# RWKV-7 recurrence inside a fused decoder layer: the second head's rows and columns swapped, its small matmuls put on the opposite quarters of the array, and the values' share of each chunk made one chunk ahead

## The chip, the cores and the metric

The kernel runs on one core of a Trainium2 chip. The metric is the device time of one execution in microseconds (us).

## What is computed

One decoder layer, in float32: sequence 1024, model width 1024. The input goes through an RMS norm and one input projection; its columns feed an RWKV-7 branch (8 heads of 64), an S5 branch and two gates; the two branches are projected, gated, merged and projected out; then a gated MLP. Most of the matrix work is large projections. The part that the change touches is the RWKV-7 recurrence:

```python
def step(S, inp):
    r_t, w_t, k_t, v_t, a_t, b_t = inp
    sa = jnp.einsum('bhij,bhj->bhi', S, a_t)
    S = (S * w_t[:, :, None, :] + sa[..., None] * b_t[:, :, None, :]
         + v_t[..., None] * k_t[:, :, None, :])
    return S, jnp.einsum('bhij,bhj->bhi', S, r_t)
```

The kernel doesn't run it step by step but in chunks of 64 steps. For one head and one chunk, with the decays folded into the factors, let A be the rows of `a` and R those of `r`, B and K the rows of `b` and `k`, V the values. Four 64x64 products of (A, R) with (B, K) make the Gram block `gr`. The block of A with B is triangular and is inverted; U solves the triangular system whose right side is A·S plus the share of the values (A·K)·V; the output is R·S + (R·B)·U + (R·K)·V; and S grows by B·U + K·V, which is one product with the stacked `UV`.

## The kernel before

**Groups and heads.** The eight heads are four pairs of pairs: the work is cut into four groups i = 0 to 3 (two groups of four heads, times two halves `th` of the sequence). In a group, `u` (0, 1) counts the two pairs of heads and `h` (0, 1) the two heads of a pair: head h of a pair holds its 64 channels on partitions 64h to 64h+63.

**Stages of a group.** `rwkv_front(d, u)` (L641) loads k, r, v and the two gates of a pair, and makes `ar` (the rows of A in columns 0 to 63 and of R in 64 to 127 of every chunk), `bk` (B and K likewise) and, with the Gram matmuls of L700 and the masking of L702, `gr`. VectorE makes the A half (L685) and the B half (L688), GpSimd the R half (L686) and the K half (L691, after its L689 and L690); VectorE's L709 makes the factor of the bonus out of the result of GpSimd's L690. `rwkv_inv` (L744) gathers the diagonal blocks of `gr` to DRAM and back (L707, L750, L762, L770, all DMAs issued on GpSimd's queue) and inverts 32x32 blocks on VectorE (L757, L759). `rwkv_nat` (L717) transposes `bk` and the values into `bkn` and the lower half of `UV`. `rwkv_level` (L772) joins the 32x32 inverses into 64x64 ones by small matmuls, L783 and L786. `rwkv_chain` (L798) runs the eight chunks, each with three segments of small matmuls:

- segment 1: L814, four products `ar`·S with a 64x128 tile of the array (64 rows of contraction, 128 columns of output; the heads use the upper and the lower row half), then L816, four products `gr`·`UV` on a 128x64 tile that add the values' share; ScalarE's L818 copies the result to `p1`;
- segment 2: L824, four 64x64 products of `gr` with `p1`, all on the same quarter; VectorE's L825 copies U into `UV`;
- segment 3: L828, four products for the output, and L832, four for the state; ScalarE's L830 copies the output to `yn`, VectorE's L835 updates S.

`rwkv_out` (L838) normalizes the output per head (VectorE, L867 last) and transposes it (L873).

**What sets the order.** TensorE's order is written by hand: `drive` (L184) interleaves three lanes, `chain_lane` (nat, level, chain, out of one group) and `prep_lane(0)`, `prep_lane(1)` (front of the next group; the second also inverts), with a background of large projections, `mm3_steps`, whose matmuls stand in L171, L172 and L173 (128x128 weights, 512 columns, three per step; called "fill" below). A lane yields the cost of what it has just issued and the time until its next step is due. Costs, pace and due times are numbers of a plan, not measured times. A lane that is not due, or whose credit is used up, lets fill steps through. When the order has been made it is fixed: TensorE runs it as written and waits where an operand isn't there. The order on the other engines comes from a scheduler that works from the same program and priorities, and every engine runs its own queue in order.

A float32 matmul shows as two instructions ("passes") in the trace, so four matmuls are a row of x8.

## Time and profile before

| | |
|---|---|
| median of three runs | 1645.7 us (1644.71 to 1648.14) |
| the profiled execution, its own time | 1647.22 us |
| its span, first to last instruction | 1645.4 us |
| mean granted TensorE clock in it | 0.963 |
| TensorE busy | 1552.2 us, 94% of the span |
| VectorE, ScalarE, GpSimd busy | 1129.1, 701.0, 146.2 us |
| RWKV stage (first matmul L666 to last transposes L873) | 278 to 846 us of the span |

Times in the trace count from the span's start. In a timeline, a row gives the start, the time from its first to its last instruction, the engine, line and operation, output<-inputs, the array tile that a matmul uses (rows*columns), the shape and count, and in brackets how long the engine had been idle before it and what ended that. Rows of neighbouring matmuls overlap, since a matmul's record lasts until its result is written, while the next one has long begun: the spacing of starts, not the length of a row, is what a matmul costs.

### The profile page before, as it was taken

What the parts mean: (1) busy time and instruction counts of PE and PEld (TensorE: products, weight loads), DVE (VectorE), ACT (ScalarE), POOL (GpSimd) and SP (SyncE); (2) the same over time, 40 slices, a digit from 0 to 9 for tenths busy, and PEclk for the clock granted to TensorE, in tenths of its full rate; (3) what the DMA queues carried; (4) which work ended last, traced back from release to release, by engine and by line L of the source; (5) the groups of instructions that cost most, each with busy time, mean ns of one, the idle gap of its engine ahead of it and who ended that gap; (6) DMA issues with size and microseconds to landing.
All of it is one profiled execution on the core that took longest, in us unless ns stands there. A gap on an engine that the chain in (4) does not pass through costs nothing. (4 is left out here: it accounts for less than half of the span.)

```text
span 1645.4 us, 22661 instructions
## 1 busy us (share of the span) xinstructions
PE 1552.2 (94%) x8372; PEld 1251.5 (76%) x8372; DVE 1129.1 (69%) x2035; ACT 701.0 (43%) x1069; POOL 146.2 (9%) x212
## 2 busy tenths in 40 slices
PE   5899899899999999989989899999999999999995
PEld 4688787687777777767778688878888888788774
DVE  6898764554364364695378668977777777788767
ACT  4345543123243243535453444544444544543451
POOL 2100101312212213111010000000000000000000
PEclk9799999998997998999999999999999999999997
DMA  5254243333333334655257344422222224862722
GB/s 174 71 146 143 88 141 136 98 115 110 94 119 103 94 119 133 156 146 156 59 174 248 128 150 151 140 92 78 77 90 78 80 96 145 296 234 86 235 89 102
DMA packets 130399, 212.59 MB, mean 129 GB/s; under 512 B 38080, under 2 KB 44224, under 8 KB 130288
## 3 DMA queue, kind: packets, MB, share of 16 engines
q1 hardware_dynamic: 120464, 181.50, 35.1%
q0 software_dynamic: 8672, 27.54, 5.5%
q10 hardware_dynamic: 1152, 2.10, 0.3%
q8 instruction: 66, 1.08, 0.3%
q14 instruction: 45, 0.37, 0.1%
HBM read 156.03 MB, written 52.95 MB: 127 GB/s over the span
## 5 line engine op out<-in xcount | busy, mean ns | idle before, releaser
L171 PE MATMUL gm<-hh,wh 128*128 128x512 f32 x688 | 301.6, 438 | 7.4 <-ACT hh L225 3.5
L172 PE MATMUL gm<-hl,wh 128*128 128x512 f32 x688 | 279.3, 406 | 5.4 <-DVE hl L226 4.5
L173 PE MATMUL gm<-hh,wl 128*128 128x512 f32 x688 | 278.5, 405 | 0.0
L156 DVE TENSOR_TENSOR wl<-wf,wh 128x512 fp32r<-128x512 f32 x179 | 123.2, 689 | 142.3 <-ACT wh L155 141.5
L155 ACT CAST wh<-wf 128x512 fp32r<-128x512 f32 x179 | 110.7, 619 | 205.3 <-PE gm L172 115.1
L171 PEld LDWEIGHTS gm<-hh,wh 128*128 128x128 f32 x688 | 134.4, 195 | 44.3 <-ACT hh L225 5.7
L172 PEld LDWEIGHTS gm<-hl,wh 128*128 128x128 f32 x688 | 135.3, 197 | 31.7 <-DVE hl L226 7.3
L173 PEld LDWEIGHTS gm<-hh,wl 128*128 128x128 f32 x688 | 134.7, 196 | 29.7
L1514 PE MATMUL d<-xl,wh 128*128 128x512 f32 x308 | 120.4, 391 | 5.7 <-DVE xl L226 5.7
L1513 PE MATMUL d<-xh,wh 128*128 128x512 f32 x308 | 120.1, 390 | 0.0
L1515 PE MATMUL d<-xh,wl 128*128 128x512 f32 x308 | 119.9, 389 | 0.0
L1339 PE MATMUL rp<-t,h 128*128 128x512 f32 x216 | 84.4, 391 | 2.3 <-ACT p L1353 1.4
L1341 PE MATMUL rp<-t,l 128*128 128x512 f32 x216 | 84.2, 390 | 0.5 <-DVE l L226 0.5
L1340 PE MATMUL rp<-t,h 128*128 128x512 f32 x216 | 84.0, 389 | 0.0
L1514 PEld LDWEIGHTS d<-xl,wh 128*128 128x128 f32 x308 | 57.8, 188 | 19.6 <-DVE xl L226 7.8
L1513 PEld LDWEIGHTS d<-xh,wh 128*128 128x128 f32 x308 | 57.8, 188 | 12.0 <-ACT q L1574 0.2
L1515 PEld LDWEIGHTS d<-xh,wl 128*128 128x128 f32 x308 | 57.8, 188 | 12.0
L225 ACT CAST h<-r 128x1024 fp32r<-128x1024 f32 x34 | 35.8, 1054 | 61.1 <-PE rp L1340 29.6
L226 DVE TENSOR_TENSOR l<-r,h 128x1024 fp32r<-128x1024 f32 x34 | 41.6, 1225 | 29.0 <-ACT h L225 27.5
L1360 DVE SCALAR_TENSOR_TENSOR y<-zv,vecs,y 128x1023 f32<-128x1023 f32 (+1 forms) x36 | 46.1, 1281 | 8.6 <-ACT y L1358 8.6
L1339 PEld LDWEIGHTS rp<-t,h 128*128 128x128 f32 x216 | 40.5, 188 | 11.8 <-ACT p L1353 2.3
L1341 PEld LDWEIGHTS rp<-t,l 128*128 128x128 f32 x216 | 40.5, 188 | 9.4 <-DVE l L226 1.0
(440 smaller groups left out, 3381.8 us busy)
## 6 DMA issues: line engine op xcount, KB each, us to landing
r<-in_w_up_dram SPq DMA_DIRECT2D x36, 512.0 KB, 3.6
wf<-in_w_in_dram SPq DMA_DIRECT2D x68, 256.0 KB, 3.0
st<-in_w_down_dram SPq DMA_DIRECT2D x55, 256.0 KB, 4.1
st<-ACT SPq DMA_DIRECT2D x44, 256.0 KB, 4.5
wf<-in_w_up_dram SPq DMA_DIRECT2D x36, 256.0 KB, 2.8
ACT<-y POOLq DMA_DIRECT2D x18, 512.0 KB, 2.9
GT<-ev SPq DMA_DIRECT2D x32, 256.0 KB, 2.1
wf<-in_w_br_dram SPq DMA_DIRECT2D x32, 256.0 KB, 3.1
```

The lines of the kernel that those rows point to most:

```text
L155: nc.scalar.copy(h[:, :n], f[:, :n])
L156: nc.vector.tensor_tensor(l[:, :n], f[:, :n], h[:, :n].bitcast(F32), ALU.subtract)
L171: mm(ps, a, xh[k], start=k == 0, stop=False)
L172: mm(ps, a, xl[k], start=False, stop=False)
L173: mm(ps, b, xh[k], start=False, stop=k == n - 1)
L1339: mm(ps, wh[:, c], xh, start=first and k == 0, stop=False, skip_group_check=True)
L1340: mm(ps, wh[:, c], xl, start=False, stop=False, skip_group_check=True)
L1341: mm(ps, wl[:, c], xh, start=False, stop=k == 3, skip_group_check=True)
L1360: V.scalar_tensor_tensor(y[:, lag:], z[:, 0:1024 - lag], self.vec(nme, i), y[:, lag:], ALU.mult, ALU.add)
L1513: mm(ps, wh[:, c], xh[:, x], start=start, stop=False, skip_group_check=True)
L1514: mm(ps, wh[:, c], xl[:, x], start=False, stop=False, skip_group_check=True)
L1515: mm(ps, wl[:, c], xh[:, x], start=False, stop=stop, skip_group_check=True)
```

## The change

For head 1 (h = 1) the two column halves of `ar`, `bk` and `gr` and the two row halves of `UV` change places: A, B and U of head 1 lie where R, K and V of head 0 lie. So a product of head 0 that uses rows 0 to 63 and columns 0 to 63 has a partner of head 1 on rows 64 to 127 and columns 64 to 127. The mask `gmask` is widened to 192 columns to serve both.

- In the front, each of the four operations that make `ar` and `bk` is cut into two, one for each head, on 64 partitions each (L688, L689, L694, L695 of the new kernel); the gather L707 and the scatter L770 become eight DMAs a group each in place of four.
- In `rwkv_nat`, the copy of the values to `UV` becomes two, a small matmul is added for the first block, and the memset of `UV` goes.
- In `rwkv_level`, the matmuls alternate between the two heads (two 32x32 tiles).
- In the chain, `ar`·S is made in two halves. Segment 1 now has the half for A (L838, four 64x64) and the values' share of the next chunk (L820, four 64x64); ScalarE's L824 keeps that share, and VectorE's L841 adds the kept share of this chunk to `ar`·S, in place of ScalarE's copy L818. Segment 2 has the four products of `gr` with `p1` (L849) and the half of `ar`·S for R (L851). Segment 3 has the four products with `UV` for the output (L856) and four for the state (L861). That is 24 matmuls a chunk for 20, all but segment 3's on 64x64 tiles. U is copied to `UV` by VectorE (L852) for head 0 and by ScalarE (L853) for head 1. A segment of four `values` matmuls is added before the first chunk.
- The plan's costs of the segments go from 1.25, 0.5 and 0.9 to 0.45, 0.45 and 0.65, those of the level from 0.4 to 0.3; so the places of all fill steps in the stage change. The number of fill matmuls doesn't.

```diff
         o = slice(d["th"] * 512, d["th"] * 512 + 512)
         p = 2 * d["g"] + u
         ar, bk = d["ar"][:, u], d["bk"][:, u]
-        ar0, ar1, bk0, bk1 = ar[:, :, 0:64], ar[:, :, 64:128], bk[:, :, 0:64], bk[:, :, 64:128]
+        ar0, ar1, bk0, bk1 = [[x[HS[h], :, HS[h ^ j]] for h in range(2)] for x in (ar, bk) for j in range(2)]
 
         gf = d["gr"][:, u].rearrange("p c h t -> p (c h t)")
         kk, yb, pe = gf[:, 0:512], gf[:, 512:1024], gf[:, 1024:1544].rearrange("p (c t) -> p c t", t=65)
@@ -682,29 +684,32 @@
         for tb in range(4):
             nc.tensor.transpose(kb[:, tb * 128:(tb + 1) * 128], yb[:, tb * 128:(tb + 1) * 128], self.cst("ident"))
         V.scalar_tensor_tensor(kk, k, self.vec("k_k", p), kb, ALU.mult, ALU.mult)
-        V.scalar_tensor_tensor(ar0, c64(kk), -1.0, pe[:, :, 0:64], ALU.mult, ALU.mult)
-        G.tensor_tensor(ar1, c64(r), pe[:, :, 1:65], ALU.mult)
+        for h, sl in enumerate(HS):
+            V.scalar_tensor_tensor(ar0[h], c64(kk)[sl], -1.0, pe[sl, :, 0:64], ALU.mult, ALU.mult)
+            G.tensor_tensor(ar1[h], c64(r)[sl], pe[sl, :, 1:65], ALU.mult)
         V.scalar_tensor_tensor(kk, ta, 1.0, kk, ALU.add, ALU.mult)
-        V.scalar_tensor_tensor(bk0, c64(kk), 0.5, c64(tz), ALU.mult, ALU.mult)
         G.tensor_scalar(ta, ta, self.ka_h[:, p:p + 1], self.ka_1[:, p:p + 1], ALU.mult, ALU.add)
         G.tensor_tensor(ta, ta, k, ALU.mult)
-        G.tensor_tensor(bk1, c64(ta), c64(tz), ALU.mult)
+        for h, sl in enumerate(HS):
+            V.scalar_tensor_tensor(bk0[h], c64(kk)[sl], 0.5, c64(tz)[sl], ALU.mult, ALU.mult)
+            G.tensor_tensor(bk1[h], c64(ta)[sl], c64(tz)[sl], ALU.mult)
         v = ld(self.RKV[8 + p])
...
-        g16 = d["gr"][:, u].rearrange("p c h t -> p (c h) t")
         for blk in range(2):
-            sl = slice(32 * blk, 32 * blk + 32)
-            nc.gpsimd.dma_start(d["md"][u, blk].rearrange("c q t -> q c t"), g16[sl, :, sl])
+            md = d["md"][u, blk].rearrange("(c h) q t -> h q c t", h=2)
+            for h in range(2):
+                sl = slice(64 * h + 32 * blk, 64 * h + 32 * blk + 32)
+                nc.gpsimd.dma_start(md[h], d["gr"][sl, u, :, h, sl])
...
                     if b == 0:
                         mm(ps[64:128, c], v[:, 0:64], ident, start=True, stop=True, skip_group_check=True)
+                        mm(ps[0:64, c], v[:, 448:512], ident, start=True, stop=True, skip_group_check=True)
                     else:
                         nc.tensor.transpose(ps[:, c], v[:, 64 * b - 64:64 * b + 64], ident)
-                A.copy(d["UV"][64:128, 4 * q:4 * q + 4, :, u], ps[64:128].rearrange("p c (h i) -> p c h i", i=64))
+                for h in range(2):
+                    A.copy(d["UV"][HS[1 - h], 4 * q:4 * q + 4, h, u], ps[HS[1 - h], :, HS[h]])
...
+        kw = dict(stop=True, skip_group_check=True)
+        steps = ((lambda u, c, h: mm(p1[u][bot[h], c], gr[top[h], u, c, h, bot[h]], xz[top[h], u, c], start=c == 0, **kw),
+                  lambda u, h: A.copy(xz[bot[h], u], p1[u][bot[h], 0:8])),
+                 (lambda u, c, h: mm(p0[u][top[h], c], xz[bot[h], u, c], gr[bot[h], u, c, h, bot[h]], start=c == 0, **kw),
+                  lambda u, h: A.copy(gr[top[h], u, :, h, bot[h]], p0[u][top[h], 0:8])))
         for step, evict in steps:
             for u in range(2):
-                for c in range(16):
-                    step(u, c)
-                    if c % 8 == 7:
-                        yield 0.4, 0.3, 2.0
-                evict(u)
+                for c in range(8):
+                    for h in range(2):
+                        step(u, c, h)
+                    if c % 4 == 3:
+                        yield 0.3, 0.3, 2.0
+                for h in range(2):
+                    evict(u, h)
             yield 0, T_LV
     def rwkv_chain(self, d):
@@ -802,38 +809,59 @@
         S, pt, UV, gr, ar, bkn = self.S[d["g"]], d["pt"], d["UV"], d["gr"], d["ar"], d["bkn"]
         d["yn"] = self.tg("yn", 1, (128, 4, 2, 2, 64))
         kw = dict(stop=True, skip_group_check=True)
-        uh = [(u, h) for h in range(2) for u in range(2)]
+        uh = [(u, h, HS[h], HS[1 - h]) for u in range(2) for h in range(2)]
+
+        def banks():
+            t = self.chk(1).rearrange("p (b e u i) -> p b e u i", b=2, u=2, i=64)
+            return t[:, 0, 0], t[:, 1, 0], t[:, 1, 1]
+
+        def values(pg, c, u):
+            for _, h, sl, ot in uh[0:2]:
+                mm(pg[sl, u], gr[ot, u, c, h, sl], UV[ot, (c + h) % 8, h, u], start=u == 0, **kw)
+
+        def keep(pg):
+            t = self.small.tile([128, 2, 64], F32, tag="p1", name=self.nm("p1"), bufs=2)
+            A.copy(t, pg)
+            return t
+        _, pg, _ = banks()
+        for u in range(2):
+            values(pg, 0, u)
+        nxt = keep(pg)
+        yield 0.3, 0
         for c in range(8):
-            py = self.chk(1).rearrange("p (h n) -> p h n", h=2)[:, :, 0:128].rearrange("p h (u i) -> p h u i", i=64)
+            pa, pg, py = banks()
+            p1 = nxt
             cb = self.chb()
-            pu = cb[0:64, 0:256].rearrange("p (h u i) -> p h u i", u=2, i=64)
-            psn = cb[:, 256:384].rearrange("p (u i) -> p u i", i=64)
+            pu, psn = [cb[:, o:o + 128].rearrange("p (u i) -> p u i", i=64) for o in (0, 256)]
             for u in range(2):
-                for h in (1, 0):
-                    sl = slice(64 * h, 64 * h + 64)
-                    mm(py[:, h, u], ar[sl, u, c], S[sl, u], start=u == 0, **kw)
-            for u, h in uh:
-                mm(py[0:64, h, u], gr[:, u, c, h, 0:64], UV[:, c, h, u], start=False, **kw)
-            p1 = self.small.tile([64, 2, 2, 64], F32, tag="p1", name=self.nm("p1"), bufs=1)
-            A.copy(p1, py[0:64])
+                for _, h, sl, ot in uh[0:2]:
+                    mm(pa[sl, u], ar[sl, u, c, sl], S[sl, u], start=u == 0, **kw)
+                if c < 7:
+                    values(pg, c + 1, u)
+            V.tensor_tensor(p1, p1, pa, ALU.add)
+            if c < 7:
+                nxt = keep(pg)
             spt = self.small.tile([128, 2, 64], F32, tag="spt", name=self.nm("spt"), bufs=1)
             for u in range(2):
                 A.mul(spt[:, u], S[:, u], pt[:, c, u:u + 1])
-            yield 1.25, T_CH
-            for j, (u, h) in enumerate(uh):
-                mm(pu[:, h, u], gr[0:64, u, c, h, 0:64], p1[:, h, u], start=j == 0, **kw)
-            V.tensor_copy(UV[0:64, c], pu)
-            yield 0.5, T_CH
-            for u, h in uh:
-                mm(py[64:128, h, u], gr[:, u, c, h, 64:128], UV[:, c, h, u], start=False, **kw)
+            yield 0.45, T_CH
+            for u, h, sl, ot in uh:
+                mm(pu[sl, u], gr[sl, u, c, h, sl], p1[sl, u], start=u == 0, **kw)
+            for u, h, sl, ot in uh:
+                mm(py[ot, u], ar[sl, u, c, ot], S[sl, u], start=c == 7 and u == 0, **kw)
+            V.tensor_copy(UV[0:64, c, 0], pu[0:64])
+            A.copy(UV[64:128, (c + 1) % 8, 1], pu[64:128])
+            yield 0.45, T_CH
+            for u, h, sl, ot in uh:
+                mm(py[ot, u], gr[:, u, c, h, ot], UV[:, (c + h) % 8, h, u], start=False, **kw)
             o = 64 * (c % 2)
-            A.copy(d["yn"][o:o + 64, c // 2].rearrange("p u h i -> p h u i"), py[64:128])
-            for u, h in uh:
-                mm(psn[64 * h:64 * h + 64, u], bkn[:, u, c, 64 * h:64 * h + 64], UV[:, c, h, u],
-                   start=u == 0 and h == 1, **kw)
+            for h in range(2):
+                A.copy(d["yn"][o:o + 64, c // 2, :, h], py[HS[1 - h]])
+            for u, h, sl, ot in uh:
+                mm(psn[sl, u], bkn[:, u, c, sl], UV[:, (c + h) % 8, h, u], start=False, **kw)
             for u in range(2):
                 V.scalar_tensor_tensor(S[:, u], psn[:, u], pt[:, c, u:u + 1], spt[:, u], ALU.mult, ALU.add)
-            yield 0.9, T_CH
+            yield 0.65, T_CH
```

**TensorE, second and third chunk of group 0 beside the front of group 1.** These are the rows before, from the third segment of the second chunk (L828, L832) on; `gm` is the output of a fill step, `rp` that of the Gram matmuls L700, `chk` and `chb` those of the chain.

```order
1313 L828 MATMUL chk_3627<-UV_3235,gr_2468 64x64 x4
1314 L832 MATMUL chb_3628<-UV_3235,bkn_3234 64x64 x4
1315 L700 MATMUL rp_3670<-ar_3332,bk_3333 128x128
...
1322 L700 MATMUL rp_3671<-ar_3332,bk_3333 128x128
1323 L171 MATMUL gm_3620<-hh_514,wh_3476 128x512
1324 L172 MATMUL gm_3620<-hl_515,wh_3476 128x512
1325 L173 MATMUL gm_3620<-hh_514,wl_3477 128x512
1326 L814 MATMUL chk_3685<-S_2462,ar_2466 128x64 x4
1327 L816 MATMUL chk_3685<-UV_3235,gr_2468 64x64 x4
```

And these are the rows after, from the same segment (L856, L861) on; L704 is the Gram matmul, L173 to L175 are fill.

```order
1322 L856 MATMUL chk_3673<-UV_3251,gr_2468 64x64 x4
1323 L861 MATMUL chb_3674<-UV_3251,bkn_3250 64x64 x4
1324 L173 MATMUL gm_3666<-hh_514,wh_3462 128x512
1325 L174 MATMUL gm_3666<-hl_515,wh_3462 128x512
1326 L175 MATMUL gm_3666<-hh_514,wl_3463 128x512
1327 L704 MATMUL rp_3726<-ar_3352,bk_3353 128x128
1328 L704 MATMUL rp_3727<-ar_3352,bk_3353 128x128
...
1334 L704 MATMUL rp_3727<-ar_3352,bk_3353 128x128
1335 L838 MATMUL chk_3738<-S_2462,ar_2466 64x64 x2
1336 L820 MATMUL chk_3738<-UV_3251,gr_2468 64x64 x2
```

The first eight Gram matmuls stood ahead of a fill step and stand behind it now; the first segment of the third chunk comes right behind them, and no fill step lies between the two.

**VectorE at the same place.** `S` is the state, `ld` the loaded inputs of the front, `bk` and `ar` its products, `UV` the copied U. Before, between the state updates (L835) of the first and the second chunk:

```order
572 L835 SCALAR_TENSOR_TENSOR S_2462<-chb_3546,pt_2469,spt_3557 128x64 x2
573 L709 SCALAR_TENSOR_TENSOR ld_3457<-ld_3457,vecs,ld_3342 128x512
574 L685 SCALAR_TENSOR_TENSOR ar_3332<-gr_3334 128x8x64
575 L688 SCALAR_TENSOR_TENSOR bk_3333<-gr_3334,ld_3340 128x8x64
576 L687 SCALAR_TENSOR_TENSOR gr_3334<-ld_3349,gr_3334 128x512
577 L688 SCALAR_TENSOR_TENSOR bk_3333<-gr_3334,ld_3347 128x8x64
578 L156 TENSOR_TENSOR wl_4001<-wf_4002,wh_4000 128x512
579 L825 COPY UV_3235<-chb_3628 64x256
580 L709 SCALAR_TENSOR_TENSOR ld_3536<-ld_3536,vecs,ld_3349 128x512
581 L835 SCALAR_TENSOR_TENSOR S_2462<-chb_3628,pt_2469,spt_3639 128x64 x2
```

After, between the same two state updates (now L863) and a little further; L714 was L709, L694 was L688, L690 was L687, L688 was L685.

```order
575 L863 SCALAR_TENSOR_TENSOR S_2462<-chb_3580,pt_2469,spt_3592 128x64 x2
576 L688 SCALAR_TENSOR_TENSOR ar_3352<-gr_3354 64x8x64 x2
577 L690 SCALAR_TENSOR_TENSOR gr_3354<-ld_3362,gr_3354 128x512
578 L841 TENSOR_TENSOR p_722_3590<-p_722_3590,chk_3673 128x128
579 L690 SCALAR_TENSOR_TENSOR gr_3354<-ld_3369,gr_3354 128x512
...
582 L852 COPY UV_3251<-chb_3674 64x128
583 L714 SCALAR_TENSOR_TENSOR ld_3506<-ld_3506,vecs,ld_3362 128x512
584 L714 SCALAR_TENSOR_TENSOR ld_3555<-ld_3555,vecs,ld_3369 128x512
585 L863 SCALAR_TENSOR_TENSOR S_2462<-chb_3674,pt_2469,spt_3686 128x64 x2
586 L694 SCALAR_TENSOR_TENSOR bk_3353<-gr_3354,ld_3367 64x8x64
587 L694 SCALAR_TENSOR_TENSOR bk_3353<-gr_3354,ld_3360 64x8x64
```

Both L714 stand now right ahead of the state update, and three of the four halves of `bk` behind it, where before all of `bk` was made ahead of it.

**GpSimd at the same place.** `ka` and `ka_h` are vectors of weights. Before, the rows that make the K half of `bk` for both pairs:

```order
62 L689 TENSOR_SCALAR ld_3342<-ld_3342,ka_h,ka_222 128x512
63 L690 TENSOR_TENSOR ld_3342<-ld_3342,ld_3338 128x512
64 L691 TENSOR_TENSOR bk_3333<-ld_3342,ld_3340 128x8x64
65 L689 TENSOR_SCALAR ld_3349<-ld_3349,ka_h,ka_222 128x512
66 L690 TENSOR_TENSOR ld_3349<-ld_3349,ld_3345 128x512
67 L691 TENSOR_TENSOR bk_3333<-ld_3349,ld_3347 128x8x64
```

And after, where L691 was L689, L692 was L690 and L695 was L691:

```order
64 L691 TENSOR_SCALAR ld_3362<-ld_3362,ka_h,ka_222 128x512
65 L692 TENSOR_TENSOR ld_3362<-ld_3362,ld_3358 128x512
66 L691 TENSOR_SCALAR ld_3369<-ld_3369,ka_h,ka_222 128x512
67 L695 TENSOR_TENSOR bk_3353<-ld_3362,ld_3360 64x8x64
68 L692 TENSOR_TENSOR ld_3369<-ld_3369,ld_3365 128x512
69 L695 TENSOR_TENSOR bk_3353<-ld_3362,ld_3360 64x8x64
70 L695 TENSOR_TENSOR bk_3353<-ld_3369,ld_3367 64x8x64 x2
```

One half of the K product (L695) stands now between the second pair's L691 and its L692, and the last three halves, instead of one whole operation, behind it.

More of the change, by code (lines that the diff above doesn't have):

```diff
@@ L27 @@
 TWO_PI = 2.0 * math.pi
+HS = (slice(0, 64), slice(64, 128))
 SIN_SCALE = 6.2831845
@@ L42 @@
 _o = 0
-for _n, _c in (("ident", 128), ("gmask", 128), ("ones_bd", 128), ("nrow", 128),
+for _n, _c in (("ident", 128), ("gmask", 192), ("ones_bd", 128), ("nrow", 128),
                ("xinit", 256), ("smask", 512)):
@@ L58, in _constants @@
     s, t = (p % 64)[:, None], (p % 64)[None, :]
-    put("gmask", np.where(p[None, :] < 64, s < t, s <= t))
+    g = np.where(p[None, :] < 64, s < t, s <= t)
+    put("gmask", np.concatenate([g, g[:, 0:64]], axis=1))
     put("ones_bd", (p[:, None] // 64) == (p[None, :] // 64))
```

28 lines of the change are left out of this document (11 added, 17 removed).

## The prediction

> **What bounds the kernel now.** I read the page first, then the table of windows over the RWKV stage.
>
> ```profile
> span 1645.4 us, 22661 instructions
> PE 1552.2 (94%) x8372; PEld 1251.5 (76%) x8372; DVE 1129.1 (69%) x2035; ACT 701.0 (43%) x1069; POOL 146.2 (9%) x212
> ```
>
> ```profile
> 389.50:399.70 10.20, 10.20 (x60) 7.88 (x57) 2.65 (x16) 1.81 (x3) 0.00 (x0) 0.50 0.22 69
> 400.00:480.00 80.00, 79.03 (x592) 59.65 (x590) 44.07 (x116) 21.81 (x51) 15.51 (x19) 1.00 0.28 83
> 700.00:740.00 40.00, 33.24 (x192) 25.45 (x191) 35.89 (x111) 15.15 (x30) 4.37 (x5) 0.91 0.53 150
> ```
>
> A window row gives its length, then busy time of PE, PEld, DVE, ACT and POOL, the granted clock, and DMA. From 400 to 480, chain of group 0 beside the front of group 1, PE has work for 79.0 of 80 us: its own work is the bound, and what a chunk no longer occupies there can be saved. From 700 to 740 DVE is the fuller engine (35.9 of 40). So PE's matmuls set the price of the gain, and the few waits that stand between them its loss. The timeline of PE shows one chunk among fill:
>
> ```profile
> 404.21 0.50 PE L828 MATMUL chk<-UV,gr 128*64 128x64 f32 x5
> ...
> 404.61 0.22 PE L832 MATMUL chb<-UV,bkn 128*64 128x64 f32 x1
> 404.61 0.22 PE L828 MATMUL chk<-UV,gr 128*64 128x64 f32 x1
> ...
> 405.06 0.50 PE L171 MATMUL gm<-hh,wh 128*128 128x512 f32 x1
> ...
> 406.66 0.66 PE L814 MATMUL chk<-S,ar 64*128 64x64 f32 x8
> 407.25 0.68 PE L816 MATMUL chk<-UV,gr 128*64 128x64 f32 x8
> 407.86 0.50 PE L171 MATMUL gm<-hh,wh 128*128 128x512 f32 x1
> 408.19 0.39 PE L172 MATMUL gm<-hl,wh 128*128 128x512 f32 x1
> 408.43 0.39 PE L173 MATMUL gm<-hh,wl 128*128 128x512 f32 x1
> ...
> 409.45 0.68 PE L824 MATMUL chb<-p,gr 64*64 64x64 f32 x8
> 410.05 0.50 PE L171 MATMUL gm<-hh,wh 128*128 128x512 f32 x1
> ```
>
> From start to start, segment 1 takes 407.86 − 406.66 = 1.20 us, segment 2 0.60, segment 3 0.85: 2.65 a chunk, 85 us over 32 chunks. L824 runs its eight passes one after another: 0.60 for eight is 0.06 a pass and about 0.14 once at the ends. L828 and L832 write different column halves, and one of each starts at the same 404.61: matmuls on different column halves overlap. L814 (two row halves, 128 columns each) takes 0.59 as L816 does with half the array.
>
> **The gain on PE.** An array quarter runs a 64x64 pass in 0.06 us. No row shows two diagonal quarters, four quarters at once, or two row halves that write one bank together, so I bound: all quarters overlap, or none. *Segment 1:* eight matmuls, sixteen passes. On four quarters four or five rounds, 0.14 + 4.5 × 0.06 = 0.40; none overlapped, sixteen rounds, 1.10. *Segment 2:* again sixteen passes, the four of `gr`·`p1` on two quarters and then the four of R on the others, so six rounds, 0.50; or sixteen, 1.10. *Segment 3:* all eight on column halves, heads alternating, eight rounds, 0.62 (before, 0.85: all four L828 stand on one half, and only the last of them overlap). Sum 1.52, against 2.65: **1.13 × 32 = 36 us**. With no overlap 2.82: 0.17 × 32 = 5 us *lost*. I take the first end, since its nearest row, L828 beside L832, shows that tiles which share nothing but rows run together, and row halves do so in L814.
>
> The Trainium skill speaks against this: "TensorEngine Tiling (Array Packing)", section "Gotcha 1: PSUM Pressure", says that different row tiles cannot access the same PSUM bank at the same time. No run here shows it so far: L814's heads write two banks, the new L838 and L849 one. By that rule the two heads of each product would go one after the other.
>
> The level's blocks:
>
> ```profile
> 511.21 0.69 PE L786 MATMUL chk<-gr,ld 32*32 32x32 f32 x16
> 511.83 0.50 PE L171 MATMUL gm<-hh,wh 128*128 128x512 f32 x1
> ```
>
> 0.62 for eight matmuls on one tile; alternating between two tiles halves the rounds, 0.41. There are 2 steps × 2 `u` × 2 blocks × 4 groups = 32: **6.7 us**, or nothing without overlap. Taken away: the `values` segment ahead of each first chunk (0.25 × 4 = 1.0) and the added matmul of `rwkv_nat` with its neighbours (0.5). Gross **41 us**.
>
> **The fronts.** Cutting an operation by partitions doubles it: time goes with the elements per partition, as ACT's copies show, and I take the same for DVE and POOL.
>
> ```profile
> L732 ACT COPY bkn<-rp 128x512 f32<-128x512 f32 x16 | 9.4, 585 | 11.9 <-PE rp L731 11.9
> L741 ACT COPY UV<-rp 64x512 f32<-64x512 f32 x16 | 9.3, 582 | 1.7 <-PE rp L740 1.3
> L689 POOL TENSOR_SCALAR ld<-ld,ka_h,ka 128x512 f32<-128x512 f32 x8 | 11.4, 1423 | 53.2 <-DVE gr L687 34.1 <-issue 19.1
> L691 POOL TENSOR_TENSOR bk<-ld,ld 128x512 f32<-128x512 f32 x8 | 10.2, 1274 | 0.6
> L707 POOL DMA_DIRECT2D md<-gr x16 | 10.6, 667 | 61.2 <-DVE gr L702 60.4 <-issue 0.7
> ```
>
> The front of group 1 lies in the first chunks of group 0. Its place in the timelines of DVE, POOL and PE:
>
> ```profile
> 405.17 0.48 DVE L835 SCALAR_TENSOR_TENSOR S<-chb,pt,spt 128x64 f32<-128x64 f32 x2
> ...
> 408.82 0.68 DVE L688 SCALAR_TENSOR_TENSOR bk<-gr,ld 128x512 f32<-128x512 f32 x1
> ...
> 413.37 1.87 DVE L709 SCALAR_TENSOR_TENSOR ld<-ld,vecs,ld 128x512 f32<-128x512 f32 x1 [1.62 <-POOL ld L690]
> 415.17 0.46 DVE L835 SCALAR_TENSOR_TENSOR S<-chb,pt,spt 128x64 f32<-128x64 f32 x2
> ```
>
> ```profile
> 412.07 1.27 POOL L690 TENSOR_TENSOR ld<-ld,ld 128x512 f32<-128x512 f32 x1
> ```
>
> ```profile
> 412.65 1.16 PE L700 MATMUL rp<-ar,bk 64*128 64x128 f32 x16
> 413.74 0.50 PE L171 MATMUL gm<-hh,wh 128*128 128x512 f32 x1
> ...
> 415.58 0.66 PE L814 MATMUL chk<-S,ar 64*128 64x64 f32 x8 [0.86 <-DVE S L835]
> ```
>
> Before, PE waits 0.86 us for a state update that is queued on DVE behind L709, which waits for POOL's L690: a chain DVE, POOL, DVE already sets this place, at the end of 9.7 us of PE work since 405.06. Replayed with the new order: the state update ends at 405.6; L688 twice (0.6 each) and L690 (0.6) let POOL start at 407.4; there L691 1.42, L692 1.27, L691 1.42, one half of L695 1.27 and L692 1.27 with gaps of 0.08 end at 414.4; the second L714 1.8, the state update 0.4, two L694 1.2: 417.8, and PE's Gram matmuls can start at about 418.4. PE's own work has shrunk by the Gram block that now stands behind the wait (1.1) and by one chunk's 1.13, and ends at 412.5. It waits **5.9 us instead of 0.86**: the first chunk's savings are turned into a wait, and the chain is itself later. Queued behind L714 on DVE are the state update and the halves of `bk`, behind these PE's Gram matmuls and the next chunk.
>
> The same replay in the other groups starts from these waits:
>
> ```profile
> 306.42 2.58 PE L700 MATMUL rp<-ar,bk 64*128 64x128 f32 x16 [5.01 <-DVE gr L702]
> ...
> 539.03 0.66 PE L814 MATMUL chk<-S,ar 64*128 64x64 f32 x8 [0.81 <-DVE S L835]
> ...
> 659.69 1.12 PE L814 MATMUL chk<-S,ar 64*128 64x64 f32 x8 [2.90 <-DVE S L835]
> ```
>
> Group 0, without a chain beside it, becomes 3.9 us later (three more halves on POOL, 1.27 each). Group 2 comes to 7.0 (+6.2). In group 3 the fill's own inputs are split on DVE behind the second L714, so that fill stops as well: 11 (+8.1). Together 3.9 + 5.1 + 6.2 + 8.1 = **23 us lost**. Bounds: if a half on 64 partitions cost half, POOL's chain would end as before and only the loss from PE's earlier arrival would be left, some 8 us; if all eight added operations on POOL and DVE a front, 8 × about 1.0, came on the path, 32 us.
>
> **The clock.** After a wait PE runs at half clock for a while:
>
> ```profile
> 304.10:311.00 6.90, 4.58 (x21) 3.96 (x22) 4.07 (x8) 0.00 (x0) 0.00 (x0) 0.51 0.24 78
> 730.80:737.60 6.80, 3.24 (x12) 2.95 (x13) 5.73 (x28) 1.89 (x3) 0.43 (x1) 0.50 0.58 193
> ```
>
> Each such stretch of 6.8 us holds the wait itself; PE's work in its rest takes double. Three waits grow beyond 5 us, each with about 4 us of such rest, 2 us dearer: **6 us lost**. From below nothing: 389.5 to 399.7 above is at 0.50 with PE busy throughout, so shorter blocks may also move a stretch away.
>
> **The output and the small edits.** DVE makes `yn` ready in L867 while fill runs:
>
> ```profile
> 477.41 1.22 DVE L867 TENSOR_TENSOR yn<-yn,rsy 128x1024 f32<-128x1024 f32 x1
> ...
> 479.22 1.04 PE L873 MATMUL rp<-csts,yn 128*128 128x128 f32 x8
> ...
> 734.36 1.97 PE L873 MATMUL rp<-csts,yn 128*128 128x128 f32 x8 [5.80 <-DVE yn L867]
> ```
>
> In group 0, 0.6 us of slack are left between its end and PE's L873, and in group 2 PE waits 5.8 already. DVE doesn't get shorter, so what the last chunks save while that chain runs becomes wait: about 1.3 a group, **5 us lost**. The eight DMAs in place of four cost POOL 4 × 0.67 × 2 more a group; the fill between output and level, 84 matmuls in the new order for 57 in the old, covers them. ACT's added copies hide behind fill (21.8 of 80 us busy). The add into `p1` and the split copy of U lie behind the two fill steps between segments, 6 × 0.23 = 1.4 us (408.19 to 408.43 is one matmul's).
>
> **Sum.** 41 − 23 − 6 − 5 = 7 us gained on the profiled execution's own 1647.2 (1.8 of which lie outside its span and stay): 1640.2. That execution was 1.5 above the median of the three runs, 1645.7, so the forecast is **1638.7 us**. What can be told from no change is 0.2%, 3.3 us.
>
> **The rivals.**
> *The waits at the fronts don't come.* If halves on POOL cost less than whole operations, 41 − 8 − 1 − 5 = 27 us are gained: 1618.7; and if the scheduler's order leaves the front's chain that much more room, 38: 1608. For it: POOL is busy for 9% of the span only. Against it: L741 beside L732. Chance 0.17.
> *Slower: the quarters don't overlap.* If two row halves cannot write one bank at the same time, the heads of one product go one after the other: segment 1 has about eight rounds (one head's A product beside the other's values), segment 2 twelve, the level gains nothing: 0.62 + 0.86 + 0.62 = 2.1 a chunk, 0.55 × 32 = 17.6 us saved, 16 after the added matmuls. The front's losses shrink since PE arrives later, to 16, the clock's to 5. Net 16 − 16 − 5 = 5 us lost: 1651. With no overlap of diagonal quarters at all, 7 + 16 + 5 = 28 lost: 1674. It decides from where the gross gain falls below about 21 us. For it: no row shows the form. Against it: the pair at 404.61. Chance 0.15. This is what the Trainium skill's "TensorEngine Tiling (Array Packing)", "Gotcha 1: PSUM Pressure", would make of the change.
> *The gathered blocks come late.* If the level waits for its added scatter DMAs in three groups, 4 × 0.67 = 2.7 us each and some clock, 9 us more are lost, and the gain is gone: 1648. Against it: the longer fill ahead. Chance 0.10.
>
> **How the numbers follow.** The forecast has 0.58 and a range of its own of 1629 to 1647 (gross 37 to 45, fronts 18 to 28, clock 3 to 8), the rivals 0.17, 0.15 and 0.10. Faster by over 0.2%: 0.52 of the forecast, 0.17, 0.02 of the last: 0.71. The same: 0.04 + 0.02 + 0.05 = 0.11. Slower: 0.02 + 0.13 + 0.03 = 0.18. The range that holds 8 in 10 takes in the first rival to its far end and the second to a little past its bank form, 1608 to 1656.
>
> **What would show it.** Right: the first segment's eight passes of L838 with L820's eight in about 0.4 us from start to start, segment 2 in 0.5, the level's blocks in 0.4; a wait of PE of about 6, 7 and 11 us ahead of L704 or L838 in the second or third chunk of groups 0, 1 and 2, ended by DVE, with L714 waiting for POOL's L692; half-clock windows behind them. Wrong: segments of 0.6 or more, with the heads' passes 0.06 apart instead of together (the second rival); PE busy through 410 to 420 (the first); a wait ahead of L783's successor ended by a DMA (the third).

## The result and the profile after

The changed kernel takes 1660.45 us (1657.75 to 1660.64, four runs) against 1645.2: a ratio of 1.0097, 95% interval 1.0079 to 1.0116. It is slower by 1%, where 7 us faster was forecast. In the traces PE is TensorE, DVE VectorE, ACT ScalarE and POOL GpSimd. The head of the profile after, busy time and share of each engine:

```profile
span 1656.0 us, 23431 instructions
...
PE 1511.4 (91%) x8644; PEld 1210.2 (73%) x8644; DVE 1155.0 (70%) x2083; ACT 714.2 (43%) x1165; POOL 180.1 (11%) x256
```

PE is busy for 40.8 us less (1552.2 before), so the gain is there; but it waits 1656.0 − 1511.4 = 144.6 us instead of 93.2. **The 41 us saved are paid back by 51 us of new waits**, 10.6 longer in all. The timeline of PE, the second chunk of group 0 (segments 1 and 2), and segment 3 of the chunk ahead of it:

```profile
407.88 0.45 PE L856 MATMUL chk<-UV,gr 128*64 128x64 f32 x8
408.16 0.40 PE L861 MATMUL chb<-UV,bkn 128*64 128x64 f32 x8
408.50 0.50 PE L173 MATMUL gm<-hh,wh 128*128 128x512 f32 x1
...
410.07 0.27 PE L838 MATMUL chk<-S,ar 64*64 64x64 f32 x2
410.08 0.27 PE L820 MATMUL chk<-UV,gr 64*64 64x64 f32 x2
410.17 0.23 PE L838 MATMUL chk<-S,ar 64*64 64x64 f32 x2
...
410.46 0.50 PE L173 MATMUL gm<-hh,wh 128*128 128x512 f32 x1
...
412.05 0.27 PE L849 MATMUL chb<-p,gr 64*64 64x64 f32 x2
412.08 0.27 PE L851 MATMUL chk<-S,ar 64*64 64x64 f32 x2
...
412.46 0.50 PE L173 MATMUL gm<-hh,wh 128*128 128x512 f32 x1
```

Segment 1 takes 0.39 us from start to start (1.20 before), segment 2 0.41, segment 3 0.62. Two L838 and two L820 start within 0.02 us: the sixteen passes of the segment go as four rounds, 0.06 to 0.11 us apart, and in each round all four quarters run at once. The two L838 of a row write one PSUM bank, at different partitions, from different row halves. The Trainium skill's "TensorEngine Tiling (Array Packing)", "Gotcha 1: PSUM Pressure", excludes that; this trace does not agree with it: with the heads one after the other the segment would have taken the 0.62 us that the prediction worked out for that rival. The level's block:

```profile
506.40 0.44 PE L790 MATMUL chb<-ld,gr 32*32 32x32 f32 x16
506.77 0.50 PE L173 MATMUL gm<-hh,wh 128*128 128x512 f32 x1
```

0.37 for 0.62. Now the waits. From 400 to 480, the window that PE filled with 79.0 of 80 us before, and from 700 to 740:

```profile
400.00:480.00 80.00, 72.02 (x658) 52.99 (x659) 47.27 (x135) 25.66 (x70) 19.67 (x24) 0.94 0.25 74
700.00:740.00 40.00, 37.38 (x320) 27.07 (x320) 29.75 (x75) 18.95 (x47) 4.09 (x8) 1.00 0.60 161
```

PE does 8 us less in the first than it could. The new waits, from PE's timeline, at the fronts of groups 0 (two rows), 1, 2 (two rows) and 3 (two rows), and at the output of group 2:

```profile
291.89 0.90 PE L685 MATMUL rp<-csts,gr 128*128 128x128 f32 x3 [4.39 <-ACT gr L683]
...
311.46 0.76 PE L704 MATMUL rp<-ar,bk 64*128 64x128 f32 x2 [7.17 <-DVE bk L694]
...
423.90 0.58 PE L704 MATMUL rp<-ar,bk 64*128 64x128 f32 x2 [6.05 <-DVE bk L694]
...
525.68 0.33 PE L838 MATMUL chk<-S,ar 64*64 64x64 f32 x2 [4.04 <-ACT p L824]
...
547.34 0.58 PE L704 MATMUL rp<-ar,bk 64*128 64x128 f32 x2 [7.47 <-DVE bk L694]
...
672.81 0.80 PE L173 MATMUL gm<-hh,wh 128*128 128x512 f32 x1 [8.40 <-ACT hh L1073]
678.41 0.79 PE L174 MATMUL gm<-hl,wh 128*128 128x512 f32 x1 [4.81 <-DVE hl L1074]
...
754.55 0.69 PE L901 MATMUL rp<-csts,yn 128*128 128x128 f32 x2 [11.10 <-DVE yn L895]
```

All waits of PE over 0.1 us at each place, summed from its timeline; "all other" is what is left of the 93.2 and 144.6 us:

| place | before | after | added | forecast |
|---|---|---|---|---|
| front of group 0 (280 to 320) | 9.4 | 16.6 | 7.2 | 3.9 |
| front of group 1 (400 to 430) | 1.0 | 8.0 | 7.0 | 5.1 |
| front of group 2 (520 to 550) | 1.0 | 12.6 | 11.6 | 6.2 |
| front of group 3 (640 to 705) | 3.7 | 17.1 | 13.4 | 8.1 |
| output of group 2 | 5.8 | 11.1 | 5.3 | } 5 |
| all other | 72.3 | 79.2 | 6.9 | } |

The front of group 1 on VectorE and GpSimd, the place that the prediction replayed:

```profile
408.70 0.47 DVE L863 SCALAR_TENSOR_TENSOR S<-chb,pt,spt 128x64 f32<-128x64 f32 x2
...
418.56 1.85 DVE L714 SCALAR_TENSOR_TENSOR ld<-ld,vecs,ld 128x512 f32<-128x512 f32 x1 [2.96 <-POOL ld L692]
420.34 0.46 DVE L863 SCALAR_TENSOR_TENSOR S<-chb,pt,spt 128x64 f32<-128x64 f32 x2
420.73 1.36 DVE L694 SCALAR_TENSOR_TENSOR bk<-gr,ld 64x512 f32<-64x512 f32 x1
422.10 1.66 DVE L694 SCALAR_TENSOR_TENSOR bk<-gr,ld 64x512 f32<-64x512 f32 x1
423.68 0.68 DVE L694 SCALAR_TENSOR_TENSOR bk<-gr,ld 64x512 f32<-64x512 f32 x1
```

```profile
417.28 1.25 POOL L692 TENSOR_TENSOR ld<-ld,ld 128x512 f32<-128x512 f32 x1
418.61 4.60 POOL L695 TENSOR_TENSOR bk<-ld,ld 64x512 f32<-64x512 f32 x3
```

The chain is as forecast link by link: L714 waits for GpSimd's L692, the state update stands behind it, and from one state update to the next 11.6 us pass (10.0 before, 11.0 in the replay). What the replay missed comes behind it. It has two halves of B (L694) at 0.6 us each ahead of the Gram matmuls; beside GpSimd's halves they took 1.36 and 1.66 us, and the third, which began when GpSimd was done, took 0.68. PE's L704 goes on at 423.90, right behind the second of them.

### The profile page after: what moved, and what is told of

The parts are those of the page before. It is cut to its first block, busy times and chain, and to the rows that moved or that the text cites. A ratio compares the mean times of both kernels' runs of the same rounds, so it can differ in the third digit from the quotient of the medians.

```text
span 1656.0 us, 23431 instructions
## 1 busy us (share of the span) xinstructions
PE 1511.4 (91%) x8644; PEld 1210.2 (73%) x8644; DVE 1155.0 (70%) x2083; ACT 714.2 (43%) x1165; POOL 180.1 (11%) x256
## 5 line engine op out<-in xcount | busy, mean ns | idle before, releaser
L173 PE MATMUL gm<-hh,wh 128*128 128x512 f32 x688 | 297.1, 432 | 16.5 <-ACT hh L1073 8.4
L175 PE MATMUL gm<-hh,wl 128*128 128x512 f32 x688 | 276.3, 402 | 0.0
L173 PEld LDWEIGHTS gm<-hh,wh 128*128 128x128 f32 x688 | 134.1, 195 | 52.4 <-ACT hh L227 9.3
L175 PEld LDWEIGHTS gm<-hh,wl 128*128 128x128 f32 x688 | 134.1, 195 | 29.1
L704 PE MATMUL rp<-ar,bk 64*128 64x128 f32 x256 | 27.6, 342 | 26.6 <-DVE bk L694 24.0
```

The lines of the kernel that those rows point to most:

```text
L173: mm(ps, a, xh[k], start=k == 0, stop=False)
L175: mm(ps, b, xh[k], start=False, stop=k == n - 1)
```

## The experiments

Theory F: the halves of the front on GpSimd and VectorE make the waits. Rivals: P, the plan's smaller costs place too few fill steps; C, the chain's new edges (ScalarE's kept copy, VectorE's add) cost what is missing. Times are medians; the kernel before stood between 1644.1 and 1644.9 beside them.

**The front whole.** The halves taken out of the changed kernel:

```diff
-        for h, sl in enumerate(HS):
-            V.scalar_tensor_tensor(ar0[h], ...)
-            G.tensor_tensor(ar1[h], ...)
+        V.scalar_tensor_tensor(ar0, c64(kk), -1.0, pe[:, :, 0:64], ALU.mult, ALU.mult)
+        G.tensor_tensor(ar1, c64(r), pe[:, :, 1:65], ALU.mult)
...
(bk0, bk1 likewise; factors of B and K times 1e-6)
```

This run leaves the swap out of the front while the chain keeps it, so its chain does the same work but it does not compute the layer; so do the later runs that build on it.

> The changed kernel with the four operations of the front that make ar and bk left whole (128 partitions, unswapped columns), and with the factors of B and K scaled by a millionth so that all numbers stay finite; the swap of head 1 is so left out of the front and the result is not the layer's. Everything else of the change stays. Theory F (the halves on GpSimd and VectorE, with L714 and the state update queued behind them, make the fronts' waits, 39 us more than before, against some 41 us saved on TensorE): the waits at the fronts of groups 1 to 3 fall from 7.6, 8.3 and 13.2 us to about 3, 3 and 6, since TensorE still comes earlier than before; total 1625 to 1635. Theory P (the smaller costs of the plan place too few fill steps ahead of every step that waits for another engine, and the halves are a small part): 1650 or more. Theory C (the new edges in the chain, ScalarE's kept copy and VectorE's add, cost what is missing): 1645 or more.

Measured 1624.5 us, ratio 0.9881 (0.9857 to 0.9906): 36 us below the changed kernel and half a microsecond below theory F's range, far from those of P and C. PE is busy for 1505.9 of 1620.8 us and waits little at the front of group 1:

```profile
402.91 0.45 PE L847 MATMUL chb<-p,gr 64*64 64x64 f32 x8 [1.36 <-DVE p L839]
...
408.94 0.27 PE L836 MATMUL chk<-S,ar 64*64 64x64 f32 x2 [0.95 <-DVE S L861]
```

So the chain and the level by themselves are worth some 20 us net, and the halves cost 36.

**The halves alone, in the old kernel.** The same four operations cut by partitions in the kernel before, columns where they were.

> The kernel before with only the four operations of the front cut into halves of 64 partitions, columns unswapped, same result; chain, level and plan as before. Theory F: the state update of the front's second chunk and the Gram matmuls come about 3 us later a front, with half clock behind some: 12 to 20 us slower than before, 1657 to 1665. If the halves hide under TensorE's longer chunks: within 4 us of before. Theories P and C: within 5 us of before.

1684.5 us, 1.0257 (1.0221 to 1.0292): 40 us slower, twice the top of the expectation. The halves are enough by themselves; no new chain is needed for their cost. In the profiled execution (1693.3 us, the longest of four) the span is 46 us longer than before: waits make 32 of it. An estimate of the clock's part: PE was busy for 123 us at half clock, as the granted clock of the trace has it, and for 98 before; half of the difference, 13 us, is lost. The wait of the changed kernel stands there, PE's timeline:

```profile
432.44 1.83 PE L703 MATMUL rp<-ar,bk 64*128 64x128 f32 x13 [6.00 <-DVE bk L693]
```

**The old plan in the new kernel.**

```diff
-            yield 0.45, T_CH
+            yield 1.25, T_CH
...
-            yield 0.45, T_CH
+            yield 0.5, T_CH
...
-            yield 0.65, T_CH
+            yield 0.9, T_CH
```

(and the level's 0.3 back to 0.4).

> The changed kernel with the plan's old costs (1.25, 0.5 and 0.9 for the segments, 0.4 for the level's blocks), so that the fill steps stand among the chain's steps about as before. Theory F: the waits move but the sum of them stays within 8 us: 1652 to 1664. Theory P: the fronts' waits fall to a third and the time to 1640 or less. Theory C: no change, 1658 to 1662.

1631.2 us, 0.9924 (0.9899 to 0.9949): 29 us below the changed kernel, the time that theory P gives. Its mechanism, fronts' waits that fall to a third, is there in part: in groups 0 to 2 they are 17.4, 5.2 and 3.0 us, for 16.6, 8.0 and 12.6 in the changed kernel. But the edit also turns the order on the other engines, whose scheduler works from the same plan. In group 1 GpSimd now makes both halves of one pair's K before it begins the other pair's:

```profile
413.66 2.96 POOL L695 TENSOR_TENSOR bk<-ld,ld 64x512 f32<-64x512 f32 x2
...
423.32 2.96 POOL L695 TENSOR_TENSOR bk<-ld,ld 64x512 f32<-64x512 f32 x2
```

VectorE's state update (420.95) stands ahead of the second L714 (423.28) there, not behind it. In group 0, where VectorE's and GpSimd's orders stay, the waits stay too. So the plan and the halves are not independent:

**Front whole and old plan.**

> Both edits together: the front's four operations whole (as in the run with the front whole, with the same scaling, and the swap left out of the front) and the plan's old costs. It completes a table of two by two in the new chain: halves and new plan 1660, whole and new plan 1624, halves and old plan 1631. If the old plan helps only because it gives the halves room (theory F, refined): whole and old plan is about the same as whole and new plan, 1615 to 1626. If the old plan is better by itself (theory P): its 29 us come on top, 1595 to 1605.

1612.75 us, 0.9810 (0.9774 to 0.9845). The old plan is worth 29 us with halves and 12 without; the halves cost 36 with the new plan and 18 with the old. Neither end of the expectation: more than half of what the plan's numbers do is there only with the halves. Whether it is room on TensorE or the order on the other engines, this table doesn't tell. The rest is elsewhere: about 6 of the 12 us stand at the output of group 2, where PE waits 11.10 us with the new costs and 5.36 with the old, the front whole in both.

**The bonus behind the halves.** L714 writes another tile, so that it can't pass the halves of B.

```diff
-        V.scalar_tensor_tensor(r, r, self.vec("r_k", p), ta, ALU.mult, ALU.mult)
+        V.scalar_tensor_tensor(tz, r, self.vec("r_k", p), ta, ALU.mult, ALU.mult)
```

> The changed kernel with L714's product written to the tile that the bk halves read, so that it cannot start ahead of them: on VectorE the state update of the second chunk no longer stands behind the second L714, and all halves of bk come earlier. Same result. Theory F with L714 as the link that passes GpSimd's delay on to the chain: the waits of groups 1 to 3 end 2 to 3 us earlier each, 1650 to 1655. If GpSimd's own halves of K, which the Gram matmuls read, are the last to come anyway: within 3 us of the changed kernel. Theories P and C: no change.

1657.4 us, 1.0076 (1.0047 to 1.0104): 3 us better, at the edge of what can be told. The Gram matmuls then wait for GpSimd's L695 itself. L714, which the prediction named as the link, passes the delay on, but taking it away frees little.

**The pairs apart.**

```diff
-        yield 0, T_LD
+        yield 0, T_LD + 6.0 * u
```

> The changed kernel, halves and new plan kept, with the second pair's lane started 6 units of the plan later (the due time behind the loads, for u = 1 only), so that GpSimd and VectorE finish the first pair's halves before the second pair's begin and a state update of the chain stands between them. Same result. Theory F1 (the halves of both pairs interleaved on GpSimd and VectorE, with the second L714 and the state update behind all of it, make the wait): the waits of 7.6, 8.3 and 13.2 us fall to 2 to 4 each, 1632 to 1643. Theory F2 (each added half costs its time wherever it stands): 1655 or more.

1656.7 us, 1.0076 (1.0048 to 1.0103). The time is theory F2's and not F1's, but the run doesn't decide between them: the waits at the Gram matmuls went, as F1 has it, and new ones came, at the second pair's transposes and in group 3. PE's timeline:

```profile
415.86 1.11 PE L685 MATMUL rp<-csts,gr 128*128 128x128 f32 x4 [6.54 <-ACT gr L683]
```

```profile
642.49 0.79 PE L173 MATMUL gm<-hh,wh 128*128 128x512 f32 x1 [12.26 <-ACT hh L227]
```

**The pairs apart, with ScalarE's help.**

```diff
-        G.tensor_scalar(ta, ta, self.ka_h[:, p:p + 1], self.ka_1[:, p:p + 1], ALU.mult, ALU.add)
+        A.activation(ta, ta, AF.Identity, bias=self.ka_1[:, p:p + 1], scale=self.ka_h[:, p:p + 1])
```

> As the run with the pairs apart, and the factor of K that GpSimd's L691 makes (1.4 us each, eight of them) made by ScalarE. Same result. Theory F1: 4 to 8 us faster than with the pairs apart alone, since GpSimd's chain ahead of the Gram matmuls is 1.4 us shorter in each pair: 1626 to 1638. If GpSimd is no longer on the path once the pairs are apart: within 3 us of that run.

1648.5 us, 1.0021 (1.0009 to 1.0034): 8 us faster than with the pairs apart alone, as expected, but 10 us above the range, since that run was too.

**The Gram matmuls due later.** Theory D, formed after the first four runs: the plan gives a front 9 units between the transposes and the Gram matmuls, and with halves it takes longer, so TensorE stands there too early.

```diff
-T_KN, T_BK, T_GR, T_INV, T_LV, T_CH, T_LN = 5.0, 9.0, 2.5, 44.0, 1.0, 0.8, 11.0
+T_KN, T_BK, T_GR, T_INV, T_LV, T_CH, T_LN = 5.0, 14.0, 2.5, 44.0, 1.0, 0.8, 11.0
```

> The changed kernel with the plan's due time between the transposes and the Gram matmuls raised from 9 to 14, nothing else: a half chunk more of TensorE's work ahead of the Gram matmuls. Same result. Theory D (the due time is too short for a front of halves, so TensorE comes to the Gram matmuls too early): the waits ahead of L704 go, 1632 to 1645. Theory F1, in which the state update's place on VectorE sets the wait: PE waits at the chunk instead, 1648 or more.

1628.8 us, 0.9905 (0.9890 to 0.9920): one number recovers 31.6 us, and the kernel is now faster than the one before by 1%. All waits over 0.3 us of PE from 400 to 430:

```profile
407.78 0.27 PE L838 MATMUL chk<-S,ar 64*64 64x64 f32 x2 [0.36 <-ACT p L824]
420.59 0.27 PE L838 MATMUL chk<-S,ar 64*64 64x64 f32 x2 [0.99 <-DVE S L863]
426.56 0.45 PE L849 MATMUL chb<-p,gr 64*64 64x64 f32 x8 [3.92 <-DVE p L841]
```

No wait stands ahead of L704 here any more: a whole chunk with its fill now lies there. PE's total wait is 122.5 us for 144.6. But the edit moves more than TensorE's arrival. In group 1 VectorE's order turned as well, and the state update no longer stands behind the second L714:

```profile
418.48 0.75 DVE L714 SCALAR_TENSOR_TENSOR ld<-ld,vecs,ld 128x512 f32<-128x512 f32 x1 [1.17 <-POOL ld L692]
...
420.17 0.46 DVE L863 SCALAR_TENSOR_TENSOR S<-chb,pt,spt 128x64 f32<-128x64 f32 x2
422.67 1.85 DVE L714 SCALAR_TENSOR_TENSOR ld<-ld,vecs,ld 128x512 f32<-128x512 f32 x1 [2.04 <-POOL ld L692]
```

In group 2 the front's operations on VectorE and GpSimd stand to one another and to the state updates as in the changed kernel, so there TensorE's order is what changed: its waits fell from 12.6 to 8.1 us, and those of the Gram matmuls (0.87 and 7.47) became 0.98 and 5.34 in the chunk that now stands there.

**The controls.** The later due time in the kernel before, and in the kernel before with halves:

> The kernel before with the due time between transposes and Gram matmuls raised from 9 to 14 and nothing else; a control for the run with the Gram matmuls due later. Same result. Theory D (a front of halves takes longer than the plan's 9, a front of whole operations about 9): the old kernel's waits at this place are 0.86, 0.81 and 2.90 us and 5.0 in group 0, so little is to be had: 0 to 8 us faster, 1637 to 1645. If the later due time is good for any kernel of this kind: 1630 or less, and the new kernel's gain by it says nothing about the halves.

1651.9 us, 1.0047 (1.0020 to 1.0073): slower by 8, where 0 to 8 faster was expected. The later due time is no gain of its own; the output of group 2 waits 10.6 us there for 5.8.

> The kernel before with the halves (1684.5 measured) and the due time raised from 9 to 14. Same result. Theory D: most of the 40 us that the halves cost is TensorE standing ahead of Gram matmuls whose operands come late, and goes with the later due time: 1645 to 1658. If the halves' time itself is on the path: 1670 or more.

1672.05 us, 1.0184 (1.0147 to 1.0221): 12 of the 40 us come back, and the time lies in the range given for the halves' own time on the path, not in theory D's. Against its own control, which is slower by 8, the halves still cost 20 us, so theory D is at most half of the story in the old chain. The kernel waits 11 us more than the control, and PE is busy for 11 more. In the new chain the later due time gives 32 us where the halves cost 36, by TensorE's order and VectorE's together; it was not tried there with the front whole, so how much of the 32 us belongs to the halves is not shown.

**Two ways on.**

> The changed kernel with the due time 14 and GpSimd's L691 made by ScalarE. Same result. Theory D with GpSimd's chain as the rest of the wait (the run with the due time alone still waits 0.99 and 3.92, 0.98 and 5.34 us for VectorE behind it): 1618 to 1626. If the rest of the wait has other causes: within 3 us of 1629.

1626.4 us, 0.9895 (0.9847 to 0.9943), the fastest kernel here that computes the layer, though not told apart from the one with the due time alone; it lies at the border of the two ranges expected and decides nothing.

> The changed kernel with the plan's old segment costs and the due time 14. Same result. If the old costs helped only by the room they gave at the fronts (theory D): no better than either alone, 1624 to 1634. If they help elsewhere too (the output of group 2 waited 11.1 us with the new costs and 5.4 with the old): 1612 to 1622.

1634.4 us, 0.9939 (0.9914 to 0.9964): the two remedies don't add up, and together are no better than either alone, as expected if they help by the same thing.

**VectorE's halves or GpSimd's.** The front whole, with only one engine's operations cut:

> The kernel with the front whole, except that VectorE's two operations a pair (A and B halves) are cut by partitions, columns unswapped; GpSimd's stay whole; same scaling and the swap left out of the front. With VectorE's halves both L714 stand ahead of the state update and three of the four B halves behind it, and GpSimd's second L692 stands behind the first pair's K operation, as in the changed kernel. Theory V (VectorE's halves turn the order round, and the order makes most of the 36 us): 1642 to 1656, most of the way from 1624.5 to 1660. Theory G (GpSimd's halves, 1.3 to 1.5 us each on the longest chain, make most): 1625 to 1635.

1645.3 us, 1.0003 (0.9988 to 1.0019).

> The same with GpSimd's two operations a pair (R and K halves) cut and VectorE's whole. The orders of VectorE and GpSimd stay as with the front whole, each GpSimd operation taking twice as long. Theory V: 1626 to 1634. Theory G: 1642 to 1656. Both alike, about 1640 each, if the two halves only add their time to one path.

1636.7 us, 0.9947 (0.9926 to 0.9968). Against 1624.5 VectorE's halves cost 21 us and GpSimd's 12, together nearly the 36. Theory V has the larger share: with VectorE's halves, the scheduler puts both L714 of group 1 ahead of the state update and most of `bk` behind it, and the waits of the changed kernel are there:

```profile
416.70 1.65 PE L704 MATMUL rp<-ar,bk 64*128 64x128 f32 x12 [4.31 <-DVE bk L694]
```

With GpSimd's alone the order of the front stays as it was. What the two do to each other shows in the rows of L694, first with VectorE's halves alone (GpSimd's operations whole), then in the changed kernel:

```profile
L694 DVE SCALAR_TENSOR_TENSOR bk<-gr,ld 64x512 f32<-64x512 f32 x16 | 10.9, 706 | 0.1
```

```profile
L695 POOL TENSOR_TENSOR bk<-ld,ld 64x512 f32<-64x512 f32 x16 | 22.9, 1433 | 1.1
L694 DVE SCALAR_TENSOR_TENSOR bk<-gr,ld 64x512 f32<-64x512 f32 x16 | 15.5, 996 | 0.1
```

0.71 us grew to 1.00 with GpSimd's halves beside them. In the time this is little: 21 and 12 make 33 of the 36 us, so at most some 3 are left for the two together.

## Why the prediction was wrong, point by point

- **The gain on PE** was right, in mechanism and in size. Segments of 0.39, 0.41 and 0.62 us for 0.40, 0.50 and 0.62; the level 0.37 for 0.41. PE's busy time fell by 40.8 us; the forecast had 41 gross. The rival in which quarters do not overlap is refuted, and with it, for row halves that write different partitions of a bank, the rule of the Trainium skill's "TensorEngine Tiling (Array Packing)", "Gotcha 1: PSUM Pressure", as a reason against the change.
- **Half operations cost whole ones**: right. L694 took 706 ns on 64 partitions (with GpSimd's operations whole) for a median of 679 on 128 with the front whole, and L695 1433 ns in the changed kernel for 1317 with the front whole.
- **The fronts** are the step that failed: "Together 3.9 + 5.1 + 6.2 + 8.1 = 23 us lost" measured 39. The mechanism, the place and, in group 1, the chain of links stand; the term was mis-sized. Of the 39, about 8 are TensorE's earlier arrival (the prediction's own lower bound, and what the run with the front whole leaves: its four fronts wait 23.5 us against 15.1 before); the halves' own part was put at 15 and is 31. The traces show three things that the replay had too small or not at all. Behind the state update, VectorE's and GpSimd's halves stretch each other (1.36 and 1.66 us for 0.6). Ahead of the place where the replay begins, there are waits that it has nowhere: in group 0 at the second pair's transposes (4.39 us at L685 for 1.16), and in group 2 at the chain's first segment (4.04 us at 525.68, 0.4 with the front whole), where ScalarE's kept copy L824 stands behind the front's L683, which waits 1.72 us for VectorE. And in group 3 the fill's own splits stop for 13.2 us, where 11 had been replayed for the whole front. How much each adds to the total was not taken apart, but for the first: the runs with one engine's halves leave some 3 us for it. The bound of 32 us that the prediction wrote down for all of it was passed, and the forecast's own range stopped at 28.
- **The clock** was put at 6 us and cost about 1. An estimate from the granted clock in the two traces: PE was busy at half clock for 98 us before and for 100 after, and half of that is lost. The half-clock stretches grew from 123 to 157 us, but what grew in them is waits; the stretch from 389.5 to 399.7, with PE busy throughout, is gone, as the prediction had thought possible.
- **The output** of group 2 lost 5.3 us. That the sum of 5 came out is luck: 1.3 us were forecast in each group, and all of it came in one. The other 7 us of waits were not forecast.
- **The sum**: 41 − 23 − 6 − 5 = 7 became 41 − 39 − 1 − 5 − 7 = −11. The slower rival had a mechanism that did not come; what came was the forecast's own loss at 1.7 times its size, to which the prediction gave 2% of its chance as a slower outcome.
- **The first rival** gave 1618.7 us for fronts without the halves' cost: the run with the front whole took 1624.5.

What stays open: how much of the halves' cost is their order on VectorE and how much their time, in either chain; how much of what the later due time and the old segment costs give is TensorE's later arrival and how much the order that they turn on the other engines; and why PE waits 6 us less at the output of group 2 with the old segment costs.

## What to carry to other kernels

When a kernel's bottleneck is made shorter, ask for each step beside it whether it was cut to the old length: here 41 us came off the busiest engine as worked out, and the engines that feed it, given more work in the same step, took them all back. Where an order is planned by due times, a change to a step's length on one engine needs its due time changed with it; one number was worth 32 us, and only with the change. Such a number can move more than it names: where a scheduler orders the other engines from the same plan, compare their order before and after it too. A loss that is worked out by replay at one place should carry its upper bound into the range.

## What the runs showed of the hardware

While GpSimd ran its halves, some of VectorE's smallest operations stopped. VectorE's timeline, group 2, and GpSimd's in the same stretch:

```profile
519.83 0.17 DVE L140 TENSOR_TENSOR rsh<-rsy 128x8 f32<-128x8 f32 x1
519.92 0.16 DVE L671 TENSOR_SCALAR sv<-rp 128x8 f32<-128x8 f32 x1
520.04 1.06 DVE L141 SCALAR_TENSOR_TENSOR rsh<-rsh,sv 128x8 f32<-128x8 f32 x1
...
521.21 1.16 DVE L138 TENSOR_SCALAR rsy<-rsy 128x8 int32<-128x8 int32 x1
```

```profile
519.88 2.46 POOL L689 TENSOR_TENSOR ar<-ld,gr 64x512 f32<-64x512 f32 x2 [2.31 <-ACT gr L677]
```

Operations of 0.17 us take 1.06 and 1.16, to the end of one GpSimd half each. The Trainium skill's "SBUF — State Buffer", "Who interferes with whom", has it that only a pair of ports shared by the two engines makes them contend, as an exclusive lock, and that a VectorE instruction with two inputs in SBUF contends with a GpSimd instruction that reads SBUF. The rows agree for L141, which reads two tiles, though not every such operation is held: an L142 that began at 521.13, together with the second half, took 0.17. L138 reads one tile, and for that the page has a stop only in the modes that use both ports, which nothing here shows. So a half on GpSimd can hold up VectorE for nearly its whole length (1.06 of 1.19 us), and since a half takes as long as a whole operation, cutting by partitions doubles the time in which this can happen.
